# A two-layer encoder trunk on one core: more weight splits finished by an accumulating DMA, the FFN forms' scaling moved behind the norm, the first norm product moved back

## The chip, the cores and the metric

The kernel runs on one core of a Trainium2 chip. A core has a matmul engine (TensorE, PE in the profile, with its weight loads as PEld), three elementwise engines (VectorE or DVE, ScalarE or ACT, GpSimd or POOL), a queue engine (SyncE or SP) and 16 DMA engines, which move data on behalf of the queues. Each engine runs its own instructions strictly in their order and waits for the others by semaphores. The metric is the time of one execution on the device, in microseconds (us), the median of several runs.

## The reference

The input x is 512 tokens of 1024 values. Each of two layers adds a mixing block and a gated MLP. Cut to what matters:

```python
for l in range(DEPTH):                                   # 2 layers, SEQ 512, D_MODEL 1024, all float32
    h = rms_norm(x, attn_norm_g[l])
    c_q, c_kv, k_rope, gq, gk, gv, pool_in, gate_logits = split_columns(h @ w_in[l], IN_SIZES)
    o_mla = mla_branch(c_q, c_kv, k_rope, ...)           # 8 heads, queries from 256 latents, keys and values from 128
    o_gqa = gqa_branch(gq, gk, gv, ...)                  # 8 heads on 2 key/value heads
    o_pool = pool_branch(pool_in, pool_w[l], pool_scale[l])
    gates = jax.nn.sigmoid(gate_logits).reshape(b, s, 3, d)
    merged = (gates[:, :, 0] * (o_mla @ w_branch_mla[l])
              + gates[:, :, 1] * (o_gqa @ w_branch_gqa[l])
              + gates[:, :, 2] * (o_pool @ w_branch_pool[l]))
    x = x + merged @ w_out[l]
    hf = rms_norm(x, ffn_norm_g[l])
    u = depthwise_conv(hf @ ffn_w_up[l], ffn_conv_w[l], ffn_conv_b[l])   # width 3, 2 x 2816 channels
    x = x + (silu(u[..., :2816]) * u[..., 2816:]) @ ffn_w_down[l]
```

## The kernel before

**Three matmuls for one.** The matmul engine reads operands in a float32 format that it rounds. So every operand is split in a high part, which is exact in that format, and a low part, which is the rest, and each product is made of three: high by high, high by low, low by high (`mm3`). The tokens stand in the free direction (512 columns); the residual `XM`, and the normed activations `HH` (high) and `HL` (low), are held as eight blocks of 128 features.

**Weights.** They come from HBM in one stream, in the order of use, cut into units (`_widths`, `_layer_units`; mostly 128x512, four blocks of 128x128). Two units lie in a `raw` tile (128x1024), and there are three such tiles. `w_split` turns a unit into `wh` and `wl`. The high part is a copy on ACT (line 297). The low part is made in one of two ways, by the unit's kind:

- kind "p": `wl = raw - wh` as one subtraction on VectorE or GpSimd (line 304); `pick` chooses the engine.
- kind "u" (`by_transfer`): ACT writes `-wh` into `wl`, then GpSimd issues a DMA that adds `raw` to it (line 435):

```python
        A.activation(hi, r, AF.Copy)
        A.activation(lo, f(hi), AF.Copy, scale=-1.0)
        nc.gpsimd.dma_start(f(lo), r, accum_op=ALU.add)
```

A unit is split some units ahead of its use (`wnext`): three ahead as a rule, four where a unit of kind "u" is near (`LA, LAP`). A `raw` tile is loaded anew when both of its units have been read (`w_free`).

**Stages of a layer.** Projection to latents, pooled channels, queries, keys and values; then attention "gqa" with the gates and products of the pool branch (2) and parts of the next as filler; attention "mla" with the rest of branch 1 and the gates of branch 0; then the products of branch 0. In the weight stream "g" is a gate's logits for 128 features (two units), "b" a branch's product (one unit), "q", "n", "v" the latent queries, keys and values. The last branch's chain for each block m is: a product with the gate (`gt`), an addition into `XM`, the split into `mgh` and `mgl`, and the load of the residual into the same place of `XM`. The output projection has eight products (m = 0 to 7) of two units each, on PSUM tags acc, ST and AV. The FFN follows: ten plain products (group 0, units of kinds "u" and "p" in turn), then products in forms: seven products of half width in the place of eight, on sums and differences of the activations that `build_forms` makes (`tt`, `tf`).

**Norms.** After each output product, `norm_steps` scales `XM` by the gain into `hn`, copies that to `HH`, squares `XM` (`sqt`), takes `HL = hn - HH`, and adds the square into `sq` on GpSimd. The `hn` are kept for the forms. When all squares are in, `norm_begin` sums them to `prt`, and `norm_finish` has PE add `prt` over the partitions in one small product into `ps_S`; from it come the factors `rt` and `rbc`, which scale results later.

**Order.** Nothing is scheduled by hand or on the chip. The program is recorded by a clock in the kernel (`Clock`) with a cost for each instruction: chains of steps are set off when the clock says that their inputs are ready, and each engine gets its instructions in that order. So a change of one cost or one step shifts others. The first norm product is recorded once `prt` has been ready for `D_SUM` on that clock.

Of the kernel before, what the change touches and what calls it, by code (L numbers as in the profile page):

```python
# [13 lines left out]
AF = mybir.ActivationFunctionType  # L14
ALU = mybir.AluOpType
# [4 lines left out]
T = 512  # L20
D = 1024
KC = D // P
# [32 lines left out]
        "mla": (-6.2, -2.9, -1.0, 0.1, 0.64, 1.678, 1.82, 35.5)}  # L55

D_ROW, D_OUT, D_IN, D_LAT = 3.4, 3.2, 4.0, 6.0
D_SUM = 2.0
D_ISSUE, D_ADD = 0.9, 4.5
REST = 0.4  # L60
W_BIAS = 2.54
# [2 lines left out]
PRM_AG, PRM_FG, PRM_PS, PRM_CQ, PRM_CKV = 0, 8, 16, 20, 22  # L64
# [11 lines left out]
def _order(br):  # L76

    r, lag = [], LAG[br]  # L80
    for m in range(KC + lag):
        r += [(k, pos.index(m)) for k, b, pos in EXTRA if b == br and m in pos]
        if m < KC:
            r.append(("g", m))
        if m >= lag:
            r.append(("b", m - lag))
    return r


WIDTHS = {"g": [T, T], "b": [T], "q": [384, 384], "n": [256], "v": [256]}  # L90
# [3 lines left out]
def _widths():  # L94

    r = [384] * KC + [T] * 8 + [T] * KC + [288] * MID + [T] + [288] * (KC - MID)
    for br in (2, 1, 0):
        late = []
        for k, _ in _order(br):
            if k in "nv":  # L100
                late = WIDTHS[k]
            else:
                r += WIDTHS[k][:1] + late + WIDTHS[k][1:]
                late = []
    return r + [T] * (2 * KC)


def _groups():
# [25 lines left out]

def _layer_units():

    r = [("p", wd) for wd in _widths()]
    for tok in _ffn():
        if tok[0] == "u":
            r += [("u", T), ("p", T), ("next",)]  # L140
        elif tok[0] == "f":
            r.append(tok)
        elif (tok[2] * SIZES[tok[1]] + tok[3]) % 4 == 0:
            r.append(("u" if tok[1] < len(SIZES) - 1 else "p", T))
    return r
# [60 lines left out]
class Clock:  # L206
# [37 lines left out]
    def done(self, *key):  # L244
        self.ready[key] = self.fin + self.SEM
# [10 lines left out]
    def chain(self, *steps, after=0.2):  # L256

        def go(n, source=None):
            if n == len(steps):
                return  # L260
            keys, fn = steps[n] if isinstance(steps[n], tuple) else ((), steps[n])
            late = [self.ready.get(k, self.now + 0.5) for k in keys]
            if late and max(late) > self.now:
                self.at(max(late) - self.now, lambda: go(n))
                return
            self.fin, self.source, self.last = self.now, source, None
            fn()
            source, self.source = self.last, None
            self.at(max(0.0, self.fin - self.now), lambda: go(n + 1, source))
        self.at(after, lambda: go(0))  # L270
# [65 lines left out]
def trunk(ctx: ExitStack, tc: tile.TileContext, x, w, prm, gb, cst, out):  # L336
    nc = tc.nc
    ctx.enter_context(tc.manual_schedule())
    ck = Clock()
    at, need, done, chain = ck.at, ck.need, ck.done, ck.chain  # L340
    V, A, G = Engine(ck, nc.vector, "DVE"), Engine(ck, nc.scalar, "ACT"), Engine(ck, nc.gpsimd, "Pool")
# [13 lines left out]
    def slot(name, dt=F32):  # L355
        uid[0] += 1
        t = sp.tile([P, SLOT], dt, tag="s", name=f"{name}_{uid[0]}")
        return t
# [31 lines left out]
    def f(ap):  # L390
        return ap.bitcast(F32)
# [145 lines left out]
    XM = cp.tile([P, KC, T], F32, tag="XM", name="XM")  # L537
# [14 lines left out]
    for l in range(L):  # L552
        t = cp.tile([P, NPRM], F32, tag=f"prm{l}", name=f"prm{l}")
# [11 lines left out]
        return steps  # L565


    def norm_steps(gen, kc, g, sq, full=None):
        xk = XM[:, kc, :]
        hh, hl = HH[:, kc, :], HL[:, kc, :]  # L570
        t = sq if kc == 0 or sq is None else slot("sqt")

        def hi():
            A.activation(hh, xk, AF.Copy, scale=g)
            if sq is not None:
                A.activation(t[:, :T], xk, AF.Square)

        def lo():
            V.scalar_tensor_tensor(hl, xk, g, f(hh), ALU.mult, ALU.subtract)
            done("H", gen, kc)  # L580

        def add():
            if kc > 0:
                G.tensor_tensor(sq[:, :T], sq[:, :T], t[:, :T], ALU.add)
            done("sq", gen, kc)

        if full is not None:
            def whole():
                full[kc] = slot("hn")[:, :T]
                V.tensor_scalar(full[kc], xk, g, None, ALU.mult)  # L590

            def hi_whole():
                A.activation(hh, full[kc], AF.Copy)
                A.activation(t[:, :T], xk, AF.Square)

            def lo_whole():
                V.tensor_tensor(hl, full[kc], f(hh), ALU.subtract)
                done("H", gen, kc)

            return [whole, hi_whole, lo_whole, add]  # L600
        return [hi, lo, add]

    def rsqrt_steps(a, n, key, eng=None):
# [24 lines left out]

    def norm_finish(gen, out, force=False):

        if gen not in parts or not (force or ck.ready.get(("prt", gen), 1e9) + D_SUM <= ck.now):
            return
        need(("prt", gen))
        s2 = ps("S")
        mm(s2[:, :16], C[:, C_GRP:C_GRP + P], parts.pop(gen), True, True)
        a, a4 = small("fac", [P, 16]), small("fac4", [P, 16])
        rt, rbc = out["rt"], out["rbc"] = small("rt", [P, 4]), slot("rbc")

        def mean():
            V.tensor_scalar(a, s2[:, :16], 1.0 / D, EPS, ALU.mult, ALU.add)  # L640
            free("S")

        def tokens():
            V.tensor_tensor(a4, a, C[:, C_SEL:C_SEL + 16], ALU.mult)
            V.tensor_reduce(rt, a4.rearrange("p (b g) -> p b g", g=4), AX.X, ALU.add)
            done("rt", gen)

        def rows():
            V.transpose(rbc[:, :T].rearrange("p (j r) -> p j r", r=32), bc(a.unsqueeze(2), [P, 16, 32]))
            done("rbc", gen)  # L650

        chain(mean, lambda: G.tensor_tensor(a, a, bc(mhalf, [P, 16]), ALU.pow), tokens, rows, after=0.3)
# [13 lines left out]
    parts = {}  # L666
# [29 lines left out]
    def layer(l, sq, xsrc):  # L696
        pr = prms[l]
        G1, G2 = 2 * l, 2 * l + 1

        def col(i):  # L700
            return pr[:, i:i + 1]
# [188 lines left out]
        for b in range(4):  # L890
            v = slot("vg", F32R)
# [704 lines left out]

        sq = slot("sq")
        tags = ("acc", "ST", "AV", "mi", "S")
        forms, whole = {}, {}

        def build_forms(q):
            a, b = whole.pop(2 * q), whole.pop(2 * q + 1)
            lo, hi = slice(0, 256), slice(256, 512)
            t = (slot("tt")[:, :T], slot("tt")[:, :T])

            def sums():
                V.tensor_tensor(t[0][:, lo], a[:, hi], a[:, lo], ALU.subtract)
                V.tensor_tensor(t[1][:, lo], b[:, hi], a[:, hi], ALU.subtract)
                V.tensor_tensor(t[0][:, hi], b[:, hi], t[0][:, lo], ALU.subtract)
                V.tensor_tensor(t[1][:, hi], b[:, lo], t[0][:, hi], ALU.subtract)  # L1610

            def halves_of(name):
                i, h = {"1": (0, lo), "2": (0, hi), "3": (1, lo), "22": (1, hi)}[name]
                d = slot("tf", F32R)[:, :T]
                forms[name, q] = d[:, lo], d[:, hi]

                def low():
                    V.tensor_tensor(d[:, hi], t[i][:, h], f(d[:, lo]), ALU.subtract)
                    done("tf", l, name, q)
                return [lambda: A.activation(d[:, lo], t[i][:, h], AF.Copy), low]  # L1620

            for name, k, h in (("11", 2 * q, lo), ("12", 2 * q + 1, lo), ("4", 2 * q + 1, hi)):
                forms[name, q] = HH[:, k, h], HL[:, k, h]
                done("tf", l, name, q)
            chain(sums, *[z for name in ("1", "2", "22", "3") for z in halves_of(name)], after=0.0)

        for m in range(KC):
            tag = tags[m % 3]
            acc = ps(tag)
            for kc in range(KC):  # L1630
                if kc % 4 == 0:
                    wh, wl = wnext()
                need(("mrg", l, kc))
                ws = slice((kc % 4) * P, (kc % 4) * P + P)
                mm3(acc, wh[:, ws], wl[:, ws], merged[kc][0][:, :T], merged[kc][1][:, :T], kc == 0, kc == KC - 1)

            def resid(m=m, acc=acc, tag=tag):
                V.scalar_tensor_tensor(XM[:, m, :], acc, 0.5, XM[:, m, :], ALU.mult, ALU.add)
                free(tag)

            chain(resid, *norm_steps(G2, m, col(PRM_FG + m), sq, whole),
                  *[lambda m=m: build_forms(m // 2)] * (m % 2))


# [8 lines left out]
        for n in range(4):  # L1653
            t = mp.tile([P, 3, T], F32R, tag="m", name=f"act{l}{n}")
# [167 lines left out]
        sq = state.get("sq")  # L1822
# [4 lines left out]
    sq = slot("sq")  # L1827
# [193 lines left out]
```

## Time and profile before

| | |
|---|---|
| time, median of 3 runs | 1562.09 us (1562.05 to 1562.57) |
| the profiled execution | 1561.47 us, of which the profile's span is 1559.7 us |
| busy in the span | PE 1543.1, DVE 1170.6, ACT 1014.1, POOL 808.6 us |
| granted TensorE clock | 1.0 throughout |
| DMA, mean share of 16 engines by queue | loads on SP 33.0%, GpSimd's 19.5% |
| layer 1: latent attention and branch 0 | about 225 to 385 us |
| output projection | 385 to 430 us, in layer 2 1160 to 1204 us |
| first FFN products | from 430 us, in layer 2 from 1204 us |

A line of the timeline reads: start, duration, engine, line of the kernel, operation, out<-in, shape, and in brackets the idle time of the engine before it with what ended it. The waits list who waited for whom: total, times, longest. A line of the stretches gives the busy time of PE, weight loads, DVE, ACT and POOL, then the granted clock, the DMA engines' mean share and GB/s.

### The profile page before, as it was taken

Reading aid. Unit: us, or ns where it says so; the run is one execution under the profiler, and the core shown is the slowest. Engines: PE = TensorE matmul, PEld = TensorE weight load, DVE = VectorE, ACT = ScalarE, POOL = GpSimd, SP = SyncE. Lnnn points to the kernel's source line nnn. Section 1 sums busy time; section 2 is a strip of 40 time slices with the busy share of each in tenths; the row PEclk is TensorE's granted clock in tenths of the full one; section 3 lists DMA queues with packets and bytes.
Section 4 is the critical chain, followed back from the end, with each engine's and each line's share of the span. In section 5 each row is a group of like instructions: output and inputs, shape, how many; then the busy total and the mean of one; then the engine's idle time right before and its main releaser. Section 6 shows DMA issues by size and latency. Waiting matters only on the chain.

```text
span 1559.7 us, 24168 instructions
## 1 busy us (share of the span) xinstructions
PE 1543.1 (99%) x8265; PEld 1340.8 (86%) x8265; DVE 1170.6 (75%) x1928; ACT 1014.1 (65%) x1914; POOL 808.6 (52%) x820
## 2 busy tenths in 40 slices
PE   9999999999999999999999999999999999999999
PEld 8888878888878999999898888788887899999997
DVE  6867886876777888877756678868767778888785
ACT  5557775773457878777644577757735577778763
POOL 3974877764653222222488648777546532222222
PEclk9999999999999999999999999999999999999999
DMA  5432224323378877876434322353143788787863
GB/s 202 123 118 82 75 88 139 116 65 128 110 174 202 193 180 170 200 189 147 128 128 131 117 75 62 101 146 113 61 139 105 181 205 194 171 192 174 213 117 102
DMA packets 124684, 216.61 MB, mean 139 GB/s; under 512 B 29328, under 2 KB 51344, under 8 KB 124560
## 3 DMA queue, kind: packets, MB, share of 16 engines
q1 hardware_dynamic: 91152, 162.93, 33.0%
q0 software_dynamic: 28512, 51.92, 19.5%
q8 instruction: 65, 1.06, 0.3%
q10 hardware_dynamic: 4896, 0.21, 0.2%
q14 instruction: 59, 0.48, 0.1%
HBM read 149.41 MB, written 13.63 MB: 105 GB/s over the span
## 4 chain that ended last, share of the span: by engine, by line
PE 86%; DVE 6%; issue 3%; ACT 2%; DMA 1%; POOL 1%; SPq 0%; ACTq 0%; POOLq 0%; DVEq 0%
PE ps_acc L523 36%; PE ps_AV L523 16%; PE ps_ST L523 14%; PE ps_S L523 10%; PE ps_mi L523 10%; DVE XM L304 1%; DVE tt L304 1%; DMA wl<-raw 1%; DVE mgl L304 1%; POOL wl L304 1%; ACT mgh L297 1%; DVE sq L304 0%; DVE gt L308 0%; ACT wh L297 0%; DVE XM L308 0%
## 5 line engine op out<-in xcount | busy, mean ns | idle before, releaser
L304 POOL TENSOR_TENSOR wl<-raw,wh 128x512 fp32r<-128x512 f32 (+3 forms) x259 | 333.2, 1293 | 274.0 <-ACT wh L297 259.0
L297 ACT ACTIVATE wh<-raw 128x512 fp32r<-128x512 f32 (+2 forms) x453 | 265.4, 605 | 49.8 <-DVE raw L304 9.9
L435 POOL DMA_DIRECT2D wl<-raw x96 | 83.7, 871 | 246.9 <-ACT sx L297 165.8
L435 POOL DMA_DIRECT2D fl<-raw x102 | 89.2, 874 | 153.9 <-ACT fl L297 67.2
L523 PE MATMUL ps_acc<-HH,wh 128*128 128x512 f32 x416 | 163.3, 393 | 4.5 <-DVE vm L304 2.9
L523 PE MATMUL ps_acc<-HH,wl 128*128 128x512 f32 x416 | 163.2, 392 | 4.1 <-DMA wl<-raw 4.1
L523 PE MATMUL ps_acc<-HL,wh 128*128 128x512 f32 x416 | 162.8, 391 | 0.2 <-DVE HL L304 0.2
L308 DVE SCALAR_TENSOR_TENSOR a<-u,prm,a 128x511 f32<-128x511 f32 x176 | 133.8, 762 | 34.9 <-ACT a L297 34.1
L312 DVE TENSOR_REDUCE nm<-ps_S 128x1 fp32r<-128x512 f32 x128 | 87.8, 686 | 37.5 <-PE ps_S L523 36.8
L297 ACT ACTIVATE a<-u,prm 128x512 f32<-128x512 f32 x88 | 71.2, 811 | 63.1 <-DVE u L304 63.1
L523 PE MATMUL ps_acc<-tf,wh 128*128 128x256 f32 x544 | 100.1, 282 | 0.0
L523 PEld LDWEIGHTS ps_acc<-HH,wl 128*128 128x128 f32 x416 | 78.1, 188 | 22.5 <-DMA wl<-raw 5.8
L523 PEld LDWEIGHTS ps_acc<-HH,wh 128*128 128x128 f32 x416 | 78.4, 188 | 21.3 <-issue 4.4
L523 PEld LDWEIGHTS ps_acc<-tf,wh 128*128 128x128 f32 x544 | 88.6, 189 | 6.2
L304 DVE TENSOR_TENSOR wl<-raw,wh 128x512 fp32r<-128x512 f32 (+2 forms) x99 | 73.3, 741 | 27.3 <-ACT wh L297 27.1
L523 PEld LDWEIGHTS ps_acc<-HL,wh 128*128 128x128 f32 x416 | 78.2, 188 | 16.5 <-DVE HL L304 0.5
L523 PE MATMUL ps_AV<-HH,wh 128*128 128x256 f32 (+1 forms) x248 | 82.3, 332 | 0.0
L523 PE MATMUL ps_AV<-HH,wl 128*128 128x256 f32 (+1 forms) x248 | 82.1, 331 | 0.0
L523 PE MATMUL ps_AV<-HL,wh 128*128 128x256 f32 (+1 forms) x248 | 82.1, 331 | 0.0
L523 PE MATMUL ps_acc<-tf,wl 128*128 128x256 f32 x272 | 76.7, 282 | 0.0
L297 ACT ACTIVATE gt<-gt 128x512 f32<-128x512 f32 x48 | 30.1, 627 | 60.2 <-DVE gt L304 60.2
L304 DVE TENSOR_TENSOR pl<-ps_ST,ph 128x512 fp32r<-128x512 f32 x86 | 58.3, 682 | 13.0 <-ACT ph L297 11.1
(428 smaller groups left out, 4999.3 us busy)
## 6 DMA issues: line engine op xcount, KB each, us to landing
raw<-w SPq DMA_DIRECT2D x160, 512.0 KB, 3.7
raw<-w SPq DMA_DIRECT2D x140, 256.0 KB, 4.3
fl<-raw POOLq DMA_DIRECT2D x102, 256.0 KB, 5.3
wl<-raw POOLq DMA_DIRECT2D x96, 256.0 KB, 4.5
raw<-w SPq DMA_DIRECT2D x14, 384.0 KB, 3.1
XM<-x SPq DMA_DIRECT2D x16, 256.0 KB, 3.5
dtq<-tr SPq DMA_DIRECT2D x16, 192.0 KB, 1.9
dtk<-tr SPq DMA_DIRECT2D x16, 192.0 KB, 2.3
```

Of the source, the lines that this page charges most:

```text
L297: return self.eng.activation(out, in_, func, **k)
L304: return self.eng.tensor_tensor(out, *a)
L308: return self.eng.scalar_tensor_tensor(out, *a)
L312: return self.eng.tensor_reduce(out, in_, *a, **k)
L435: nc.gpsimd.dma_start(f(lo), r, accum_op=ALU.add)
L523: PE.matmul(o, lhsT=lhsT, rhs=rhs, start=start, stop=stop, skip_group_check=again)
```

## The change

It makes three edits.

1. More units are of kind "u": the gates and products of branch 0, of branch 1 the latent values "v" and the gates m = 1 to 3, and all 16 units of the output projection. That is 48 units a layer. They are split four units ahead instead of three.
2. `norm_steps` no longer makes `hn`. `HH` is a copy of `XM` with the gain as its scale, and `HL` is one operation from `XM`, the gain and `HH`. `build_forms` makes the two `hn` that it needs itself, 2.0 us later on the recording clock.
3. The norm product of the first norm waits for `D_FIRST` = 2.4 instead of 2.0 on that clock.

```diff
-D_SUM = 2.0
+D_SUM, D_FIRST = 2.0, 2.4
...
-        for k, _ in _order(br):
+        for k, m in _order(br):
+            added = k in "gb" and br == 0 or br == 1 and (k == "v" or k == "g" and 1 <= m <= 3)
+            ws = [("u" if added else "p", wd) for wd in WIDTHS[k]]
...
-    return r + [T] * (2 * KC)
+    return r + [("u", T)] * (2 * KC)
...
-    def norm_steps(gen, kc, g, sq, full=None):
+    def norm_steps(gen, kc, g, sq):
...
-            def whole():
-                full[kc] = slot("hn")[:, :T]
-                V.tensor_scalar(full[kc], xk, g, None, ALU.mult)
-
-            def hi_whole():
-                A.activation(hh, full[kc], AF.Copy)
-                A.activation(t[:, :T], xk, AF.Square)
-
-            def lo_whole():
-                V.tensor_tensor(hl, full[kc], f(hh), ALU.subtract)
...
-            return [whole, hi_whole, lo_whole, add]
         return [hi, lo, add]
...
         def build_forms(q):
-            a, b = whole.pop(2 * q), whole.pop(2 * q + 1)
+            a, b = slot("hn")[:, :T], slot("hn")[:, :T]
+            def whole():
+                for k, z in ((2 * q, a), (2 * q + 1, b)):
+                    V.tensor_scalar(z, XM[:, k, :], col(PRM_FG + k), None, ALU.mult)
...
-            chain(sums, *[z for name in ("1", "2", "22", "3") for z in halves_of(name)], after=0.0)
+            chain(whole, sums, *[z for name in ("1", "2", "22", "3") for z in halves_of(name)], after=2.0)
```

Three places of the recorded order, in each of which lines of the kernel after are three higher than before. The first is PE in the second pooled channel's product, at the start of layer 1 (`ps_S<-prt` is the norm product). Before:

```order
L523 MATMUL ps_AV_388<-HL,wh_324 128x512
L523 MATMUL ps_AV_388<-HH,wl_325 128x512
L523 MATMUL ps_S_396<-prt_169,C 128x16
L523 MATMUL ps_AV_388<-HH,wh_324 128x512
L523 MATMUL ps_AV_388<-HL,wh_324 128x512
L523 MATMUL ps_AV_388<-HH,wl_325 128x512
```

And now:

```order
L526 MATMUL ps_AV_388<-HH,wh_324 128x512
L526 MATMUL ps_AV_388<-HL,wh_324 128x512
L526 MATMUL ps_AV_388<-HH,wl_325 128x512
L526 MATMUL ps_S_399<-prt_169,C 128x16
L526 MATMUL ps_AV_388<-HH,wh_324 128x512
```

The norm product has moved behind three matmuls of the product that it interrupts.

The second is VectorE in the first attention, at the first latent values of layer 1 (`vm`; their product is in `ps_acc`, `pl` and `vt` belong to the softmax). Before:

```order
L304 TENSOR_TENSOR pl_2296<-ps_mi_2289,ph_2295 128x512
L320 CAST vm_2326<-ps_acc_2316 128x4x64
L308 SCALAR_TENSOR_TENSOR vt_2211<-ps_ST_2277,vg_73_587,vt_2211 128x512
L304 TENSOR_TENSOR wl_2337<-raw_2160,wh_2336 128x512
L308 SCALAR_TENSOR_TENSOR vt_2211<-ps_mi_2289,vg_73_587,vt_2211 128x512
L304 TENSOR_TENSOR vm_2324<-ps_acc_2316,vm_2324 128x4x63
L304 TENSOR_TENSOR vm_2326<-ps_acc_2316,vm_2326 128x4x63
```

And now:

```order
L307 TENSOR_TENSOR pl_2288<-ps_mi_2283,ph_2287 128x512
L323 CAST vm_2332<-ps_acc_2325 128x4x64
L323 CAST vm_2334<-ps_acc_2325 128x4x64
L311 SCALAR_TENSOR_TENSOR vt_2220<-ps_mi_2283,vg_73_587,vt_2220 128x512
L307 TENSOR_TENSOR vm_2332<-ps_acc_2325,vm_2332 128x4x63
L307 TENSOR_TENSOR vm_2334<-ps_acc_2325,vm_2334 128x4x63
```

The subtraction for a weight unit is gone from the row, one `vt` stands earlier, and both copies of the values are VectorE's.

The third is GpSimd from the end of the output projection into the FFN's first units (`DMA wl` issues a transfer; `sq` adds a square). Before:

```order
L304 TENSOR_TENSOR wl_4501<-raw_4371,wh_4500 128x512
L304 TENSOR_TENSOR wl_4537<-raw_4422,wh_4536 128x512
L304 TENSOR_TENSOR sq_4267<-sq_4267,sqt_4498 128x512
L304 TENSOR_TENSOR wl_4561<-raw_4422,wh_4560 128x512
L435 DMA wl_4565<-raw_4485 128x512
L304 TENSOR_TENSOR sq_4267<-sq_4267,sqt_4558 128x512
L304 TENSOR_TENSOR wl_4610<-raw_4485,wh_4609 128x512
```

And now:

```order
L438 DMA wl_4546<-raw_4486 128x512
L438 DMA wl_4576<-raw_4486 128x512
L307 TENSOR_TENSOR sq_4307<-sq_4307,sqt_4543 128x512
L438 DMA wl_4606<-raw_4534 128x512
L307 TENSOR_TENSOR wl_4630<-raw_4534,wh_4629 128x512
L307 TENSOR_TENSOR sq_4307<-sq_4307,sqt_4603 128x512
```

The FFN's first transfer (`wl_4565` before, `wl_4606` now) has no weight subtraction in front of it any more, and the projection's own units are transfers.

More of the change, by code (lines that the diff above doesn't have):

```diff
@@ L96, in _widths @@
     r = [384] * KC + [T] * 8 + [T] * KC + [288] * MID + [T] + [288] * (KC - MID)
+    r = [("p", wd) for wd in r]
     for br in (2, 1, 0):
         late = []
-        for k, _ in _order(br):
+        for k, m in _order(br):
+            added = k in "gb" and br == 0 or br == 1 and (k == "v" or k == "g" and 1 <= m <= 3)
+            ws = [("u" if added else "p", wd) for wd in WIDTHS[k]]
             if k in "nv":
-                late = WIDTHS[k]
+                late = ws
             else:
-                r += WIDTHS[k][:1] + late + WIDTHS[k][1:]
+                r += ws[:1] + late + ws[1:]
                 late = []
-    return r + [T] * (2 * KC)
+    return r + [("u", T)] * (2 * KC)
 def _groups():
@@ L135, in _layer_units @@
 def _layer_units():
-    r = [("p", wd) for wd in _widths()]
+    r = _widths()
     for tok in _ffn():
@@ L585, in add @@
             done("sq", gen, kc)
-        if full is not None:
-            def whole():
-                full[kc] = slot("hn")[:, :T]
-                V.tensor_scalar(full[kc], xk, g, None, ALU.mult)
-            def hi_whole():
-                A.activation(hh, full[kc], AF.Copy)
-                A.activation(t[:, :T], xk, AF.Square)
-            def lo_whole():
-                V.tensor_tensor(hl, full[kc], f(hh), ALU.subtract)
-                done("H", gen, kc)
-            return [whole, hi_whole, lo_whole, add]
         return [hi, lo, add]
@@ L629, in norm_finish @@
     def norm_finish(gen, out, force=False):
-        if gen not in parts or not (force or ck.ready.get(("prt", gen), 1e9) + D_SUM <= ck.now):
+        if gen not in parts or not (force or ck.ready.get(("prt", gen), 1e9) + (D_SUM if gen else D_FIRST) <= ck.now):
             return
@@ L1598, in layer @@
         tags = ("acc", "ST", "AV", "mi", "S")
-        forms, whole = {}, {}
+        forms = {}
         def build_forms(q):
-            a, b = whole.pop(2 * q), whole.pop(2 * q + 1)
+            a, b = slot("hn")[:, :T], slot("hn")[:, :T]
             lo, hi = slice(0, 256), slice(256, 512)
             t = (slot("tt")[:, :T], slot("tt")[:, :T])
+            def whole():
+                for k, z in ((2 * q, a), (2 * q + 1, b)):
+                    V.tensor_scalar(z, XM[:, k, :], col(PRM_FG + k), None, ALU.mult)
             def sums():
@@ L1639, in resid @@
                 free(tag)
-            chain(resid, *norm_steps(G2, m, col(PRM_FG + m), sq, whole),
+            chain(resid, *norm_steps(G2, m, col(PRM_FG + m), sq),
                   *[lambda m=m: build_forms(m // 2)] * (m % 2))
```

## The prediction

> **What bounds the kernel now.** I read the page first, then the waits of PE, then the timeline at each wait, and last the queues behind it.
>
> ```profile
> PE 1543.1 (99%) x8265; PEld 1340.8 (86%) x8265; DVE 1170.6 (75%) x1928; ACT 1014.1 (65%) x1914; POOL 808.6 (52%) x820
> L304 POOL TENSOR_TENSOR wl<-raw,wh 128x512 fp32r<-128x512 f32 (+3 forms) x259 | 333.2, 1293 | 274.0 <-ACT wh L297 259.0
> L435 POOL DMA_DIRECT2D wl<-raw x96 | 83.7, 871 | 246.9 <-ACT sx L297 165.8
> ```
>
> PE is busy for 99%, and the change takes no matmul away. So there is nothing to win but the time in which PE stands still, and the question is which of its waits the change ends. The waits of PE name them:
>
> ```profile
> PE ps_acc L523 <- DMA wl<-raw: 4.1, 4, 2.5
> PE ps_acc L523 <- DVE vm L304: 2.9, 2, 1.5
> PE ps_acc L523 <- ACT HH L297: 1.2, 1, 1.2
> PE ps_S L523 <- DVE prt L312: 1.0, 1, 1.0
> PE ps_acc L523 <- DVE mgl L304: 0.5, 2, 0.2
> ```
>
> These five make 9.7 us of idle time in the two layers. A record of a matmul overlaps the next one, so I take the loss from starts: in an unbroken stretch starts are 0.227 apart, as 204.71 to 204.94 below shows, and a record is 0.39 long. A wait thus costs about 0.16 more than the idle time in its bracket. The timeline of PE at the waits:
>
> ```profile
> 29.22 0.39 PE L523 MATMUL ps_AV<-HH,wl 128*128 128x512 f32 x1
> 30.62 0.39 PE L523 MATMUL ps_S<-prt,C 128*128 128x16 f32 x2 [1.01 <-DVE prt L312]
> ...
> 204.71 0.39 PE L523 MATMUL ps_acc<-HL,wh 128*128 128x512 f32 x1
> 204.94 0.39 PE L523 MATMUL ps_acc<-HH,wl 128*128 128x512 f32 x1
> 206.78 0.47 PE L523 MATMUL ps_acc<-HH,wh 128*128 128x512 f32 x1 [1.46 <-DVE vm L304]
> ...
> 385.06 0.39 PE L523 MATMUL ps_acc<-oh,wl 128*128 128x512 f32 x1
> 385.58 0.47 PE L523 MATMUL ps_acc<-mgh,wh 128*128 128x512 f32 x1
> ...
> 390.46 0.39 PE L523 MATMUL ps_acc<-mgh,wh 128*128 128x512 f32 x1
> 391.09 0.50 PE L523 MATMUL ps_acc<-mgl,wh 128*128 128x512 f32 x1 [0.23 <-DVE mgl L304]
> ...
> 430.00 0.39 PE L523 MATMUL ps_acc<-HL,wh 128*128 128x512 f32 x1
> 431.46 0.50 PE L523 MATMUL ps_acc<-HH,wl 128*128 128x512 f32 x1 [1.07 <-DMA wl<-raw]
> ...
> 435.69 0.39 PE L523 MATMUL ps_acc<-HH,wl 128*128 128x512 f32 x1
> 437.29 0.49 PE L523 MATMUL ps_acc<-HH,wh 128*128 128x512 f32 x1 [1.21 <-ACT HH L297]
> 438.02 0.50 PE L523 MATMUL ps_acc<-HL,wh 128*128 128x512 f32 x1 [0.23 <-DVE HL L304]
> ```
>
> **The change part by part.** The first norm product (A) waits at 30.62, and PE loses 30.62 - 29.22 - 0.23 = 1.17. It now stands three matmuls later, which fill 3 x 0.227 = 0.68 of that; their operands are the same tiles that PE reads right after the wait today. The sum that it waits for comes no sooner, so 0.49 stays. Gain 0.68; it lies between 0 and 1.17.
>
> The values of the latent keys (B): at 206.78 PE loses 1.84 - 0.23 = 1.61 until VectorE's vm frees the bank. What VectorE did in front of it:
>
> ```profile
> 203.61 1.57 DVE L304 TENSOR_TENSOR wl<-raw,wh 128x512 fp32r<-128x512 f32 x1
> 205.77 0.87 DVE L304 TENSOR_TENSOR vm<-ps_acc,vm 128x252 fp32r<-128x252 f32 x4
> ```
>
> The subtraction of 1.57 goes to a transfer, so the four vm end about 1.5 sooner, near 205.1, and PE wants the bank at 205.17. The wait goes, in both layers (the waits have it twice, 2.9 in all): 2 x 1.61 = 3.2. Less comes only if the second half of the values, which the order puts behind one more transpose, is late instead; it has a whole gate between its product and the next user of its bank. Between 0 and 3.2; I take 3.2.
>
> The end of the third branch (C): 385.58 - 385.06 - 0.23 = 0.29 and 391.09 - 390.46 - 0.23 = 0.40, 0.69 a layer, 1.4 in two. The last link is an addition on VectorE beside a subtraction on GpSimd:
>
> ```profile
> 387.24 0.69 DVE L304 TENSOR_TENSOR mgl<-XM,mgh 128x512 fp32r<-128x512 f32 x1
> 387.85 1.80 DVE L304 TENSOR_TENSOR XM<-XM,gt 128x512 f32<-128x512 f32 x1
> ...
> 387.81 1.29 POOL L304 TENSOR_TENSOR wl<-raw,wh 128x512 fp32r<-128x512 f32 x1 [1.81 <-ACT wh L297]
> ```
>
> The same form with nothing on GpSimd takes 0.69. With a transfer in the place of the subtraction the link is 1.1 shorter, more than the 0.69 that PE waits. Between 0 and 1.4; I take 1.4.
>
> The entry into the FFN (D): 431.46 - 430.00 - 0.23 = 1.23, then 438.02 - 435.69 less two pitches = 1.88, and in the second layer the longest wait for wl, 2.5 + 0.16 = 2.7: 5.8 in all. The causes in the first layer:
>
> ```profile
> 422.63 0.63 ACT L297 ACTIVATE wl<-wh 128x512 fp32r<-128x512 f32 x1
> 423.72 1.48 POOL L304 TENSOR_TENSOR wl<-raw,wh 128x512 fp32r<-128x512 f32 x1
> 425.14 1.06 POOL L435 DMA_DIRECT2D wl<-raw  x1
> ...
> 423.97 1.51 DVE L316 TENSOR_SCALAR hn<-XM,prm 128x512 f32<-128x512 f32 x1
> 435.31 0.68 DVE L308 SCALAR_TENSOR_TENSOR XM<-ps_ST,XM 128x512 f32<-128x512 f32 x1
> 436.09 0.49 DVE L316 TENSOR_SCALAR hn<-XM,prm 128x512 f32<-128x512 f32 x1
> ```
>
> The first transfer of the FFN was ready for issue at 423.3, stood behind a subtraction until 425.14, and PE started 6.3 later. The subtraction is gone, so it leaves at 423.3 at the latest and lands by 429.6, before 430.23. The last XM ran at 435.31 though the matmuls before 430.00 had fed it: VectorE was 5 behind, with scalings of 0.49 stretched to 1.51 beside GpSimd. Both causes of the lag go: GpSimd subtracts less, and ACT's HH no longer waits for hn. XM then ends near 430.7 and HH near 431.4, three before the 434.7 at which it is wanted once the 1.23 is gone. The second layer repeats the order. What is late next is the transfer. Between 0 and 5.8; I take 5.8.
>
> Two later waits for wl (E) are what is left of 4.1 in the waits after 1.1 and 2.5: 0.5, with 2 x 0.16 about 0.9. They sit behind ACT's and VectorE's work on the first FFN products, which starts sooner. I take half, 0.4.
>
> The forms' scaling itself costs nothing: VectorE does the same 0.49 and 0.69 for each part, the scaling only later, and the forms are first read after ten products of 24 matmuls, 54 us on. The first norm's sum is built as before.
>
> The sum of gains: 0.7 + 3.2 + 1.4 + 5.8 + 0.4 = 11.5.
>
> Now what it adds. 96 subtractions (88 on GpSimd, 8 on VectorE) become an ACT pass of 0.63 and a GpSimd issue of 0.87. The new wait is GpSimd's for ACT's second pass; behind it stand the additions of squares and of the heads' outputs, which nobody reads within a microsecond. On SP weight loads move in front of residual loads that they stood behind, which costs nothing, as the residual is read a whole product later. GpSimd gains 88 x 1.29 - 96 x 0.87 = 30 us, which is worth nothing by itself. ACT gains 96 x 0.63 = 61 us of work, beside the softmax of the latent attention most of all:
>
> ```profile
> 150.00:180.00 30.00, 29.71 (x138) 24.41 (x137) 25.24 (x42) 24.37 (x46) 26.08 (x31) 1.00 0.29 84
> 290.00:353.00 63.00, 63.00 (x275) 52.31 (x274) 47.09 (x76) 45.58 (x84) 42.89 (x38) 1.00 0.24 78
> ...
> L297 ACT ACTIVATE wh<-raw 128x512 fp32r<-128x512 f32 x13 | 8.1, 623 | 0.3 <-issue 0.3
> ```
>
> In 290 to 353 ACT is busy 45.6 of 63 and PE never stands still. Its thirteen units, the last row, make 13 x 0.63 = 8.2 more, 53.8, 85%. The nearest row is 150 to 180, with ACT at 81% and PE short of 0.29 in 30; for 63 us that is 0.6 a layer, 1.2 in two (F). The ends are 0 and one pass of 0.63 late for each of 16 heads, 10.
>
> The DMA engines (G). Shares of the queues in 430 to 470, and landings there:
>
> ```profile
> q1 hardware_dynamic: 1799, 5.01, 43.9%
> q0 software_dynamic: 1028, 1.88, 26.6%
> ...
> raw<-w SPq DMA_DIRECT2D x7, 512.0 KB, 4.1
> wl<-raw POOLq DMA_DIRECT2D x7, 256.0 KB, 6.0
> ```
>
> A transfer of 256 KB takes 0.266 x 40 / 7 = 1.5 of all engines, a load of 256 KB 0.439 x 40 / 19 = 0.9. In the last products of the third branch and in the output projection a unit lasts 12 x 0.227 = 2.72, and 24 such units now follow each other: 2.4 in 2.72, and 3.3 while the residual is loaded as well (eight units). That piles up 8 x 0.6 = 4.8. The lead is four units, 10.9, less 0.63 + 0.63 + 0.87 + 6.0, which leaves 2.8 spare. So PE loses between 0 and 2.0 a layer; I take 0.6, 1.2 in two, since residual loads can wait.
>
> Net 11.5 - 2.4 = 9.1. The profiled execution took 1561.47, 0.62 under the median of 1562.09: 1552.4 by its own time, 1553.0 as a median.
>
> **The rivals.** *PE still finds its next wait.* A PE that is ahead of its feeders waits at the next one. For it: every wait named is the end of a chain that started long before. Against it: in 290 to 353 PE lost nothing. If half the gains go so: 1562.1 - 5.7 + 2.4 = 1558.8.
>
> *The transfer at the FFN's entry is as late as now*, held by the 24 in front of it. Then D and E give nothing: 1562.1 - 5.3 + 2.4 = 1559.2.
>
> *ACT becomes the bound of the latent attention*, at the far end of F: 1562.1 - 11.5 + 10 + 1.2 = 1561.8. Against it stand the 63 - 53.8 = 9 us in which ACT would still be idle there.
>
> *Slower: the raw tiles run out.* There are three, of two units each, and a tile is now held until its second transfer has landed. One round is 4.1 + 0.63 + 0.63 + 0.87 + 6.0 + 2.72 = 15.0, and three tiles cover 6 x 2.72 = 16.3. It decides once the two landings together exceed 11.4 (10.1 now). At 5 and 9 a round is 18.9, 2.6 too long; four rounds in two layers are 21, with D and E lost: 1562.1 - 5.3 + 21 = 1578. For it: the share of 3.3 in 2.72 above. Against it: residual loads end after eight units.
>
> *The issue is held up by VectorE.* The issue at 425.14 began while the hn of 423.97 ran, and took 1.06 against the mean of 0.87. Two hn now stand back to back, 0.98; four pairs in each of two layers, each with an issue that PE awaits, would cost 7.8: 1560.8. The spare 2.8 of the lead speaks against it. The Trainium skill, page "SBUF — State Buffer", section "🔬 SBUF: two separate sides", has a rule for this: while VectorE runs a two-port fp32 operation, GpSimd can't write the descriptors of its DMAs. By that rule every issue would wait for the whole pair; the row above shows only 0.19.
>
> **How the numbers follow.** The forecast of 1553.0 (1549.7 to 1557) has 0.58; half the gains 0.12; the late entry 0.11; ACT 0.08; the raw tiles 0.08; the held issue 0.03. The lowest time is all of A to E with no cost, 1.17 + 3.22 + 1.38 + 5.76 + 0.87 = 12.4, hence 1549.7. The upper end, 1559.5, takes in the half and the late entry. About 0.2%, 3.1 us, is what a measurement here can tell from no change: under 1559.0 is faster. Forecast, the half and part of the late entry make 0.77; ACT, the held issue and the rest make 0.15; the tiles 0.08.
>
> **What would show it.** Right: no wait for vm and none for HH; prt at about 0.3; the XM additions at 0.69; transfers of the output projection landing within 8. Wrong: waits for wl between 365 and 430, ACT waiting for raw, or PE idle in 290 to 353; with more than 6 us of these the forecast falls.

## The result, and the profile after

The kernel after takes 1551.81 us (median, 1550.60 to 1553.75), the kernel before beside it 1562.33 (1562.05 to 1562.95): 10.5 less, a ratio of 0.9933 with a 95% interval of 0.9916 to 0.9951. The forecast was 1553.0, the range 1549.7 to 1559.5. The profiled execution took 1550.60, with a span of 1548.8, against 1561.47 before.

The page after, its first line and the groups that changed places:

```profile
PE 1542.1 (100%) x8265; PEld 1341.3 (87%) x8265; DVE 1156.3 (75%) x1936; ACT 1066.5 (69%) x1994; POOL 775.3 (50%) x828
L438 POOL DMA_DIRECT2D wl<-raw x192 | 172.4, 903 | 383.1 <-ACT sx L300 163.7
L307 POOL TENSOR_TENSOR wl<-raw,wh 128x512 fp32r<-128x512 f32 (+2 forms) x171 | 219.9, 1294 | 179.4 <-ACT wh L300 171.7
```

ACT has 52 us more work, GpSimd 33 less, and PE's busy time is what it was. What went is PE's waiting. The waits of PE after (total, times, longest):

```profile
PE ps_mi L1835 <- DVE keep L335: 1.1, 1, 1.1
PE ps_S L526 <- DVE prt L315: 0.6, 2, 0.4
PE ps_S L526 <- DVE nm L315: 0.6, 2, 0.3
PE ps_acc L526 <- DVE XM L311: 0.4, 1, 0.4
PE ps_acc L526 <- DVE HL L311: 0.3, 1, 0.3
```

Wl, vm, mgl and HH are gone from this list; 9.7 us of named waits have become 0.9 (prt and HL). Added up over all starts of matmuls, without those of the first microseconds, which come at about half the pace in both, gaps of more than 0.12 above the pitch made about 17 us before and 5.5 after. The difference of some 11 accounts for the change of the span, 10.9.

PE's timeline at the first norm product, and at the end of the first FFN product:

```profile
29.04 0.39 PE L526 MATMUL ps_AV<-HH,wl 128*128 128x512 f32 x1
29.80 0.40 PE L526 MATMUL ps_S<-prt,C 128*128 128x16 f32 x2 [0.36 <-DVE prt L315]
...
430.88 0.39 PE L526 MATMUL ps_acc<-HH,wl 128*128 128x512 f32 x1
431.41 0.50 PE L526 MATMUL ps_acc<-HH,wh 128*128 128x512 f32 x1
432.19 0.50 PE L526 MATMUL ps_acc<-HL,wh 128*128 128x512 f32 x1 [0.28 <-DVE HL L311]
...
435.95 0.39 PE L526 MATMUL ps_ST<-HH,wl 128*128 128x512 f32 x1
436.61 0.40 PE L526 MATMUL ps_S<-prt,C 128*128 128x16 f32 x2 [0.27 <-DVE prt L315]
```

The first norm product loses 29.80 - 29.04 - 0.23 = 0.53 instead of 1.17. At 431.41 PE still loses 0.30 on HH, at 432.19 another 0.55 on HL, and at 436.61 it loses 0.43 on the second norm product, which lost nothing before. In layer 2 the same three places lose 0, 0 and 0.21.

### The profile page after: what moved, and what is told of

Read it like the earlier page. It is cut to its first block, busy times and chain, and to the rows that moved or that the text cites. A ratio compares the mean times of both kernels' runs of the same rounds, so it can differ in the third digit from the quotient of the medians.

```text
span 1548.8 us, 24353 instructions
## 1 busy us (share of the span) xinstructions
PE 1542.1 (100%) x8265; PEld 1341.3 (87%) x8265; DVE 1156.3 (75%) x1936; ACT 1066.5 (69%) x1994; POOL 775.3 (50%) x828
## 4 chain that ended last, share of the span: by engine, by line
PE 92%; DVE 3%; DMA 2%; ACT 1%; issue 1%; POOL 1%; SPq 0%; ACTq 0%; POOLq 0%; DVEq 0%
PE ps_acc L526 40%; PE ps_AV L526 17%; PE ps_ST L526 15%; PE ps_S L526 10%; PE ps_mi L526 9%; DMA raw<-w 1%; DVE tf L307 1%; ACT wh L300 0%; SPq L862 0%; POOL wl L307 0%; DVE ctl L311 0%; DVE win L307 0%; ACT mx L300 0%; DVE wl L307 0%; POOL fac L307 0%
## 5 line engine op out<-in xcount | busy, mean ns | idle before, releaser
L438 POOL DMA_DIRECT2D wl<-raw x192 | 172.4, 903 | 383.1 <-ACT sx L300 163.7
L307 POOL TENSOR_TENSOR wl<-raw,wh 128x512 fp32r<-128x512 f32 (+2 forms) x171 | 219.9, 1294 | 179.4 <-ACT wh L300 171.7
L300 ACT ACTIVATE wl<-wh 128x512 fp32r<-128x512 f32 x192 | 120.6, 628 | 6.1
L307 DVE TENSOR_TENSOR wl<-raw,wh 128x512 fp32r<-128x512 f32 (+2 forms) x91 | 66.2, 729 | 22.9 <-ACT wh L300 22.7
```

The lines of the kernel that those rows point to most:

```text
L300: return self.eng.activation(out, in_, func, **k)
L307: return self.eng.tensor_tensor(out, *a)
```

## The experiments

Each kernel is the one before or the one after with one edit, the last with two. In the diffs `p` is the split by subtraction, `u` the one by transfer. Differences of medians are against the kernel before measured beside it (1561.7 to 1562.0).

**Each part alone.** The kernel before with only the projection's units by transfer:

```diff
-    return r + [("p", T)] * (2 * KC)
+    return r + [("u", T)] * (2 * KC)
```

> The kernel before, with the 16 units of the output projection made by transfer and nothing else changed. Theory (each wait goes with the edit that took away its own cause): the two waits for wl at the FFN's entry go (1.23 + 2.65) and most of the 0.9 after them, the waits for HH and HL (1.88) stay within 0.5; 4.3 us less than before. Rival 1 (the transfer is held by the 16 in front of it on GpSimd's queue): the waits stay, -0.5 to +1 us. Rival 2 (VectorE's lag goes with GpSimd's subtractions alone): the 1.88 goes as well, 6.2 us less.

Measured: 1553.76 against 1562.02, 8.3 less (ratio 0.9948, 0.9935 to 0.9960). The waits of PE in it:

```profile
PE ps_acc L526 <- DVE vm L307: 2.9, 2, 1.5
...
PE ps_acc L526 <- ACT HH L300: 1.0, 2, 0.7
PE ps_S L526 <- DVE prt L315: 0.9, 1, 0.9
...
PE ps_acc L526 <- DVE HL L307: 0.5, 2, 0.2
```

All four waits for wl are gone: 1.23 + 2.65 + 0.9. HH and HL do not simply stay: they fall from 1.88 to 0.92 in layer 1, and where there was no loss in layer 2 there is now 1.40. This is PE finding its next wait, on a small scale. What I had not expected is that gt and mgl are gone too, so the 1.4 of the third branch belongs to this edit as well.

Branch 0's 24 units a layer alone:

```diff
+            added = k in "gb" and br == 0
```

> The kernel before, with only the gates and products of branch 0 (24 units a layer) made by transfer. Theory: the XM additions at the end of the third branch fall from 1.80 to 0.69 and the waits for gt and mgl go: 1.4 us less, nothing lost. Rival (the DMA engines of this stage saturate): waits for wl between 355 and 430 us, 1 to 2 us a layer, so 0 to 3 us more than before.

Measured: 1560.38 against 1562.02 (ratio 0.9992, 0.9983 to 1.0001), 1.6 less, not separated from no change. The waits for gt and mgl are gone, and no wait for wl stands between 355 and 429 us, so there is nothing for the rival. The theory holds for the waits, but only in part for the additions: of the last four in layer 1 the last takes 0.69, and the three before it 1.08, 1.78 and 1.08, beside subtractions that are now those of the projection's first units.

Branch 1's eight units a layer alone:

```diff
+            added = br == 1 and (k == "v" or k == "g" and 1 <= m <= 3)
```

> The kernel before, with only the latent values and the gates 1 to 3 of branch 1 (8 units a layer) made by transfer. Theory: the two waits for vm go, 3.2 us less. Rival 1 (ACT's eight more passes a layer fall on the softmax): PE waits for ACT or for the scores between 160 and 225 us, so 1.5 to 2.5 us less only. Rival 2 (the second half of the values is late instead): a new wait of PE for vm, under 1 us less.

Measured: 1558.06 against 1562.02, 4.0 less (ratio 0.9978, 0.9969 to 0.9988). The waits for vm are gone from both layers, and between 163 and 383 us no gap is over 0.17. That is the theory, and neither rival.

The forms' scaling alone (the edits of `norm_steps` and `build_forms`):

> The kernel before, with only the forms' scaling moved out of the norm's chain. Theory (HH of the last block waited for hn): the wait for HH and HL falls from 1.88 to under 0.9, the waits for wl stay; 1.0 to 1.9 us less. Rival (what is late is XM itself, behind VectorE's operations that GpSimd's subtractions stretch): the 1.88 stays within 0.5, no change that can be measured.

Measured: 1560.66 against 1562.02 (ratio 0.9992, 0.9983 to 1.0000). PE loses 1.12 on HH and 0.56 on HL in layer 1, against 1.38 and 0.50: the rival's case, HH did not wait for hn but for XM. Neither theory had the rest: the waits for wl fell as well, from 1.23 to 0.37 and from 2.65 to nothing, and in layer 2, where HH and HL had cost nothing, 1.13 and 0.56 took their place.

**Which of the two latent units?** In the kernel before, only "v" by transfer:

```diff
+            added = br == 1 and k == "v"
```

> The kernel before, with only the latent values of branch 1 (2 units a layer) by transfer. Theory (the 1.57 in front of vm is the subtraction of one of the gates' units behind the values): the waits for vm (1.61 each) stay, within 1 us of before. Rival (the subtraction is that of the values, or the order turns on them): the waits go, 3.2 us less.

Measured: 1564.61 against 1562.04, 2.6 more (ratio 1.0019, 1.0010 to 1.0028). The waits of PE in it:

```profile
PE ps_acc L526 <- DMA wl<-raw: 3.5, 4, 1.7
PE ps_ST L526 <- DMA qb<-nm: 3.3, 2, 1.7
PE ps_acc L526 <- ACT HH L300: 2.0, 2, 1.5
...
PE ps_acc L526 <- ACT ph L300: 0.6, 2, 0.4
```

The waits for vm go even here, and a loss of 0.57 and 0.39 on ph takes their place. But 1.78 and 1.87 on qb come 11 us later, a small transfer from ACT's own queue. So my theory falls, and the rival is half right: two units end the wait for vm, but they shift ACT so that another comes due. The eight units of the change do not have it. Why not is a matter of the recorded order, which I did not take apart.

**Which of the projection's units?** The last four alone, and the first twelve alone:

```diff
+    return r + [("p", T)] * (2 * KC - 4) + [("u", T)] * 4
...
+    return r + [("u", T)] * (2 * KC - 4) + [("p", T)] * 4
```

> The kernel before, with only the last four of the projection's 16 units by transfer. Theory (GpSimd's queue in front of the FFN's first transfers is what counts): the waits for wl at the FFN's entry (1.23 + 2.65) go as with all 16, those for gt and mgl (1.4) stay; 4 us less than before. Rival (all 16 count, since GpSimd and VectorE carry a lag from product to product): the waits for wl stay above 1 in each layer, under 2 us less.

Measured: 1555.69 against 1562.04, 6.3 less (ratio 0.9959, 0.9947 to 0.9972). All waits for wl are gone, gt and mgl stay, and HH and HL fall to 0.50 in each layer. That is the theory, and more than it promised. The profiled execution took 1558.32, 2.6 above the median: it loses 1.94 on the first norm product, in front of all changed units.

> The kernel before, with only the first 12 of the projection's 16 units by transfer. Theory: the XM additions at the end of the third branch fall to 0.69 and the waits for gt and mgl (1.4) go, since the subtractions beside them were those of the projection's units; the waits for wl at the FFN's entry stay above 1 in each layer; 1.4 to 2.5 us less. Rival (the lag, above): the waits for wl go here as well, 5 us or more less.

Measured: 1558.62, 3.4 less (ratio 0.9979, 0.9970 to 0.9989). Its waits:

```profile
PE ps_acc L526 <- ACT HH L300: 5.2, 2, 3.2
...
PE ps_acc L526 <- DMA wl<-raw: 0.4, 1, 0.4
```

Gt and mgl are gone, as expected: the subtractions beside the XM additions were those of the projection's first units. The waits for wl went as well but for 0.52 in layer 2, which I had not expected. The loss on HH is now 2.17 and 3.35, since VectorE begins its last XM 4.9 after PE has entered the FFN. The profiled execution took 1562.01, 3.4 above the median, at a mean clock of 0.998. So it shows where PE waits, and not the 3.4 by which the median fell. VectorE in this kernel in front of the last XM:

```profile
426.06 1.97 DVE L307 TENSOR_TENSOR tt<-hn,tt 128x256 f32<-128x256 f32 x2
427.95 0.68 DVE L311 SCALAR_TENSOR_TENSOR XM<-ps_acc,XM 128x512 f32<-128x512 f32 x1
...
430.68 2.83 DVE L307 TENSOR_TENSOR tf<-tt,tf 128x256 fp32r<-128x256 f32 x2
433.43 0.68 DVE L311 SCALAR_TENSOR_TENSOR XM<-ps_ST,XM 128x512 f32<-128x512 f32 x1
```

Beside GpSimd's work these two pairs take 1.97 and 2.83; without it they take 0.87 (kernel after) and 0.75 (forms later), as rows below show. So the entry into the FFN has two feeders, the transfer and VectorE's lag, and the one that comes last is what PE waits for. Transfers in the place of the last four subtractions help both.

**The forms from the other side.** The kernel after with the forms' edit undone, and the kernel after with the forms built later (the diff is the second's):

```diff
-            chain(whole, sums, *[z for name in ("1", "2", "22", "3") for z in halves_of(name)], after=2.0)
+            chain(whole, sums, *[z for name in ("1", "2", "22", "3") for z in halves_of(name)], after=8.0)
```

> The kernel after, with the forms' scaling put back into the norm's chain. Theory (the forms' edit is worth what HH's wait for hn is worth once the transfer is on time): in the kernel with the projection alone PE lost 0.92 in layer 1 and 1.40 in layer 2 on HH and HL, in the kernel after 0.86 and 0 and 0.64 on the two norm products; so 0.8 to 1.5 us more than after. Rival (the transfers alone do it, as VectorE is free of stretched operations): within 0.3 us of after.

Measured: 1550.72 against 1561.71 (ratio 0.9926, 0.9914 to 0.9938). The kernel after has 0.9933, 0.9916 to 0.9951: the edit gains nothing that can be measured. PE loses 0.72 and 0.71 on HH and HL in the two layers, and nothing on the second norm product.

> The kernel after, with the forms built 8.0 instead of 2.0 later on the recording clock. Theory (the last XM stands behind two hn of 0.88 and sums of 1.52, 1.51 and 0.87 on VectorE that GpSimd stretches, so it is 3.2 late): the last XM comes within 1 us of its product, the waits for HH, HL (0.86) and prt (0.43 and 0.21) go, 1.5 us less than after. Rival (the squares' additions on GpSimd set prt): HH and HL go but prt stays, 0.9 less. Rival (forms become late for the first product in forms): a wait for tf some 54 us later, more than after.

Measured: 1555.43 (ratio 0.9961, 0.9949 to 0.9972), about 3.6 more than the kernel after. The last XM comes only 0.5 sooner (3.1 after the FFN's entry instead of 3.6), since a stretched pair of tf stands in front of it now, and the two hn have moved between it and the sum of squares. VectorE in it:

```profile
431.05 0.75 DVE L311 SCALAR_TENSOR_TENSOR HL<-XM,prm,HH 128x512 fp32r<-128x512 f32 x1 [0.79 <-ACT HH L300]
431.72 2.97 DVE L319 TENSOR_SCALAR hn<-XM,prm 128x512 f32<-128x512 f32 x2
...
436.81 0.69 DVE L315 TENSOR_REDUCE prt<-sqT 128x16 f32<-128x512 f32 x1
437.41 0.75 DVE L307 TENSOR_TENSOR tf<-tt,tf 128x256 fp32r<-128x256 f32 x2
```

The pair of hn takes 2.97 here, against 0.88 in the kernel after. PE loses 1.02 and 1.26 on the norm product and 0.81 and 1.55 on wl some 25 us later. This is none of my three cases: for the norm product, the moved work met the next chain, not the forms' own. What made the later transfers for wl late I did not follow.

**The two costs and the slower rival.** All 96 units of the branches by transfer, and two raw tiles instead of three:

```diff
+            added = k in "gbvqn"
...
-RAW = 3
+RAW = 2
```

> The kernel after, with all units of the three branches' part of the stream by transfer (96 a layer instead of 48). It prices the costs F and G. Theory (ACT's passes fall beside the softmax): between 160 and 225 us ACT is busy 52 of 65 and takes 12 more, so it is full there, and PE loses 2 to 6 us over both layers. Rival 1 (the DMA engines' share, 0.92 of the output projection, reaches the branches): waits for wl, 4 us or more. Rival 2 (both costs stay nothing as long as no engine is full): within 1 us of after.

Measured: 1572.36 against 1561.71 (ratio 1.0067, 1.0053 to 1.0081), 20 us more than the kernel after. Its longest waits of PE:

```profile
PE ps_ST L526 <- DMA qa<-nm: 2.9, 2, 1.7
PE ps_S L531 <- DVE gk L307: 2.4, 1, 2.4
PE ps_S L526 <- DVE nm L315: 2.0, 2, 1.0
...
PE ps_acc L526 <- DVE MQ L323: 1.9, 2, 0.9
```

So the cost exists, but not as either theory had it. ACT was busy 57.6 of 65 between 160 and 225 us, not full; only 0.7 was waited for wl. PE waits for small links of other chains (scores' maxima, the scaling of keys, latents) that share ACT, GpSimd and VectorE with the splits. The DMA engines are a fourth candidate: the two transfers of qa that PE waited for took 5.7 and 6.3 to land, where the longest in the kernel after took 4.1. Which of the four makes each link late is not settled.

> The kernel after, with two raw tiles instead of three. It prices the rival that the raw tiles run out. By its sum one round of a tile is 15.0, two tiles cover 4 x 2.72 = 10.9, so each round of four units loses 4.1; six rounds a layer in branch 0's last products and the projection: 45 to 50 us more than after, with PE waiting for raw or wl there. Rival (the two landings overlap with the tile's other unit, and the round is short): under 10 us more.

Measured: 1611.80 (ratio 1.0318, 1.0302 to 1.0334), 60 more than the kernel after. PE's clock and longest waits:

```profile
core 0: 1608.9 us, clock 0.992
PE ps_acc L526 <- ACT MQ L300: 7.7, 2, 4.1
PE ps_ST L526 <- DMA wl<-raw: 6.7, 5, 2.1
PE ps_acc L526 <- ACT HH L300: 5.5, 2, 2.8
```

The gaps of more than 0.12 make about 51 here, some 45 more than in the kernel after, against 45 to 50 by the sum of a tile's round. Most of the rest is new: 12.1 us (0.4 in the kernel after) come from 76 matmuls that started at about half the pace, 0.427 apart instead of 0.227 where they have 512 columns. The size is that of the sum, the place is not: only 18 of the 51 (8.5 and 9.3 in the two layers) lie in branch 0's last products and the projection. MQ's 7.7 lies near 104 and 905 us, where all units are subtractions, which that sum left out; near 104 ACT stood 4.78 waiting for a load into a raw tile, and MQ comes behind that split in its order. So the raw tiles do run out at two, and that the size agrees is in part luck.

**Without the parts that gave nothing.** The kernel after without the forms' edit and without branch 0's units:

```diff
-            added = k in "gb" and br == 0 or br == 1 and (k == "v" or k == "g" and 1 <= m <= 3)
+            added = br == 1 and (k == "v" or k == "g" and 1 <= m <= 3)
```

> The kernel after without the forms' edit and without branch 0's units: the projection's 16, branch 1's 8 and the first norm product stay. Theory (branch 0's transfers are worth nothing beside the projection's, as either ends the waits for gt and mgl): within 1 us of the kernel without the forms' edit (1550.7), no wait of PE between 353 and 430. Rival 1 (branch 0's own): the 1.4 returns. Rival 2 (the crowd of transfers on the DMA engines cost something): 1 us or more less.

Measured: 1549.18 against 1562.04, 12.9 less (ratio 0.9916, 0.9902 to 0.9929). It has the lowest median of all kernels here, with half of the added transfers. The projection and branch 1 alone make 8.3 + 4.0, and the first norm product 0.6: the same 12.9. So branch 0's units and the forms' edit seem to cost 2.4 (12.9 less 10.5) between them. The intervals of this kernel and the kernel after overlap, so that cost is likely but not shown.

## Why the prediction was right

The total and its sign came out, B and C by their own steps, and A in its direction. D and both costs did not, and their errors cancelled: D gave 1.5 less than forecast, and the costs were 2.2 lower. Another 1.3 of the difference between the two profiles is chance at the start. So that the total came so close is partly luck.

A, the first norm product: 0.68 forecast, 1.17 - 0.53 = 0.64 measured. That the two agree is in part luck: the sum did come sooner, prt ending at 29.74 instead of 30.57. In the profiles of the eight kernels whose norm product is not moved, with the same matmuls up to it, the loss lies between 0.34 and 1.94; in the six in which it is moved, between 0 and 0.53. So the gain is there, but one pair of profiles doesn't give its size.

B, the latent values: 3.2 and 3.2; the four vm now end at 202.3, and PE goes on in ps_acc at 204.03 without a gap:

```profile
201.40 0.87 DVE L307 TENSOR_TENSOR vm<-ps_acc,vm 128x252 fp32r<-128x252 f32 x4
...
203.80 0.39 PE L526 MATMUL ps_ST<-qb,kb 65*128 65x512 f32 x1
204.03 0.40 PE L526 MATMUL ps_acc<-HH,wh 128*128 128x512 f32 x1
```

C, the third branch: 1.4 and 1.4, and the additions take 0.69 as foretold. Only the owner was not unique: branch 0's transfers end the waits alone, and so do the projection's.

```profile
381.50 0.69 DVE L307 TENSOR_TENSOR XM<-XM,gt 128x512 f32<-128x512 f32 x1
```

The Trainium skill, page "SBUF — State Buffer", section "Who interferes with whom", says that a VectorE operation with two inputs in SBUF contends with a GpSimd operation that reads SBUF, and that a scaling such as hn contends when it runs in a two-port mode. The traces agree on the first: the addition takes 1.80 beside a subtraction and 0.69 without one. They fit the second: two hn take 2.97 where GpSimd's addition of a square began just before them, and 0.88 where they began first; in which mode they ran no trace shows.

D, the entry into the FFN: 5.8 forecast, 4.3 measured (1.82 in layer 1, 2.44 in layer 2). The transfer's part held: no wait for it is left. The step that failed is "both causes of the lag go". VectorE in the kernel after, in front of the last XM, and ACT behind it:

```profile
425.46 0.88 DVE L319 TENSOR_SCALAR hn<-XM,prm 128x512 f32<-128x512 f32 x2
426.26 1.52 DVE L307 TENSOR_TENSOR tt<-hn 128x256 f32<-128x256 f32 x1
427.70 1.51 DVE L307 TENSOR_TENSOR tt<-hn,hn 128x256 f32<-128x256 f32 x1
429.13 0.87 DVE L307 TENSOR_TENSOR tt<-hn,tt 128x256 f32<-128x256 f32 x2
429.92 0.68 DVE L311 SCALAR_TENSOR_TENSOR XM<-ps_ST,XM 128x512 f32<-128x512 f32 x1
...
430.63 0.72 ACT L300 ACTIVATE HH<-XM,prm 128x512 fp32r<-128x512 f32 x1 [2.35 <-DVE XM L311]
```

GpSimd beside them:

```profile
425.89 1.60 POOL L307 TENSOR_TENSOR wl<-raw,wh 128x512 fp32r<-128x512 f32 x1 [1.96 <-ACT wh L300]
427.46 1.46 POOL L307 TENSOR_TENSOR sq<-sq,sqt 128x512 f32<-128x512 f32 x1
```

XM ended at 430.60, near the forecast 430.7, but PE had come to the FFN 3.4 us sooner (at 426.35 instead of 429.77; a part of this is the chance at the start, below), so it wanted HH at 431.1, not at 434.7. I had set a time from the old clock against a need that the same gains move forward. VectorE begins the last XM 3.6 after PE has entered the FFN, against 5.5 before (435.31 - 429.77), because the forms' hn and sums stand in front of the last XM, and GpSimd still subtracts every second FFN unit and adds the squares beside them: two sums of 128x256 take 1.52 and 1.51, where two others take 0.87 together. That HH waited for hn was the wrong half of the cause: the forms' edit alone moved it by 0.2.

E, the two later waits for wl: 0.4 taken, 0.9 measured. They went whole, the upper end.

F and G, the costs: 1.2 and 1.2 taken, 0 and at most 0.2 measured (0.17 on a form's transfer near 500 us). The stretches say so:

```profile
290.00:353.00 63.00, 63.00 (x275) 52.30 (x274) 46.25 (x75) 50.78 (x92) 34.79 (x37) 1.00 0.58 138
353.00:385.00 32.00, 32.00 (x142) 26.27 (x141) 21.32 (x34) 21.61 (x39) 10.02 (x12) 1.00 0.87 208
385.00:430.00 45.00, 45.00 (x201) 37.26 (x200) 29.21 (x42) 29.50 (x54) 23.33 (x23) 1.00 0.92 217
```

PE is busy throughout, with ACT at 81% and the DMA engines at 92%; the projection's transfers landed within 6.9. Taking the 0.6 of a stretch with another mix of work for a price was the mistake: here these high shares have no wait behind them, and cost nothing. That it can cost is what the kernel with all units by transfer shows, only elsewhere.

What the sum did not have: 1.3 at the start, where the profiled execution of before lost 0.66 and 0.67 at 8 us on the first weights. In the other kernels' profiles, whose start is the same, this loss lies between 0 and 1.1, so it is chance. Three small new gaps (0.26, 0.20 and 0.17) stand against it. By the profiles: 0.64 + 3.23 + 1.37 + 4.26 + 0.88 + 1.33 - 0.63 = 11.1, against 10.9.

Of the rivals, "PE still finds its next wait" happened on a small scale, as HL and the second norm product. The late entry did not: the first FFN transfer left 9.4 us ahead of PE. The raw tiles held at three and failed at two, at nearly the price worked out but mostly in other places. The held issue: the mean rose from 871 to 903 ns, and PE waited for none.

## What to carry to other kernels

When several waits of the bound engine are removed, each later need moves forward by all the gains in front of it; a feeder's time must be compared with the new need, not the old one. Ask which feeder comes second at the place of each wait: here the transfer and VectorE's lag stood behind one another, and the last four units in front of the place were enough to help both. Take the parts apart afterwards: half of this change gave nothing beside the rest, and the kernel without it had the lowest median.

## What the runs showed of the hardware

**A wait can cost more than itself.** In the kernel with the forms' edit alone PE waited 1.12 and 0.56 us near 1210, and then started eight matmuls 0.427 apart instead of 0.227, 1.6 us more. The stretches there (the granted clock is the third number from the end):

```profile
1206.00:1210.00 4.00, 2.94 (x11) 1.58 (x9) 3.54 (x6) 2.02 (x5) 2.09 (x2) 1.00 0.74 228
1210.00:1212.00 2.00, 1.72 (x7) 1.39 (x7) 1.93 (x3) 1.97 (x5) 1.87 (x2) 0.77 0.80 234
1212.00:1215.00 3.00, 3.00 (x10) 2.33 (x9) 2.96 (x5) 0.29 (x1) 1.66 (x2) 0.58 0.59 96
```

It doesn't happen every time, and not by the length of the wait alone: in the profile of before, 1.38 and 0.50 at 437 and 2.65 at 1207 were followed by nothing of the kind. It did happen after 1.94 at 30 us in the kernel with the projection's last four units, and after 1.87 at 991 us in the kernel with the values alone.

One such stretch of 1.6 us is 0.1% of an execution, which fits a mean clock of 0.999 instead of 1.000. Of 57 runs of the kernel before, 40 had a mean clock of 0.998 or 0.999, with a median of 1562.3, and 17 had 1.000, with a median of 1560.5. The kernels with the projection, with branch 1, without the forms' edit and the last one had 1.000 in all of their 24 runs. The kernel after had it in three of four, and the fourth, at 0.999, took 1553.75. So up to 1.7 us of a difference between medians may be the clock's; the 10.9 between the two profiles, both at 1.0, holds none of it. Which waits set it off isn't shown: the kernel with branch 1 alone still loses between 1.2 and 1.4 at each of four waits at the FFN's entries, and had 1.000 throughout.

The Trainium skill, page "TensorE: Matmul & The Clock Gate", section "HAM oscillation — how this bites in real kernels", gives gaps of over about 3.4 us as what lowers the clock; here two waits of 1.12 and 0.56, and single ones of 1.87 and 1.94, were followed by it, so in this case shorter waits can be enough.
